# Gating a result one product later in the mix stage, and VectorE kept to the written order of these steps

## The chip, the core and the metric

The kernel runs on one core of a Trainium2 chip. The metric is the device time of one execution in microseconds (us), and the time of a kernel is the median of its runs. The engines that matter here are TensorE (PE in the profile; PEld is its loading of weights), VectorE (DVE), ScalarE (ACT), GpSimd (POOL), and SyncE (SP, whose queue issues nearly all of the transfers; SPq is that queue). PSUM is the memory that TensorE adds its products into, in eight banks of 128 x 512 fp32.

## What is computed

One layer of a decoder, 2048 rows of 1024 fp32 values. Two mixers read the same modulated input, their gated results are merged, projected and normalized:

```
a = sliding_window_sink_attention(q, k, v, ...) * silu(a_gate);  a = a @ w_attn_proj
p = pooled(p_in) * pool_scale * silu(p_gate);                    p = p @ w_pool_proj
y = sigmoid(m_a) * a + sigmoid(m_p) * p
y = (y @ w_out) * (1 + gate)
x = layer_norm(alpha * x + y, gain, bias)
```

The change lies in the third of these lines: in the products with `w_attn_proj` and `w_pool_proj`, and in the multiplications with sigmoid(m_a) and sigmoid(m_p) that use up their results.

## The kernel before

**Products.** Every fp32 matrix is held as a high part and a low part in TensorE's fp32r type, and a product is three passes: high by high, high by low, low by high. A *quad* is two blocks of 128 output columns by two halves of 512 rows, computed by a scheme of seven block products instead of eight. They are called B11, T1, T2, B21, T3, B22 and T4 after the set of input sums that each reads (`sets[name]`). Each is twelve matmuls of 128x128 by 128x512. A quad accumulates in three PSUM banks: a and b (tag `mm`, four banks) and c (tag `lg`, two banks).

**Groups.** Quads go through TensorE in pairs, called a group: x0 and x1. `front` writes B11 and T1 of both quads. `back` then writes T2 and B21 of x0, T2 and B21 of x1, T3 and B22 of x0, T3 and B22 of x1, T4 of x0 and T4 of x1; then the next group's `front` follows. So a group is fourteen products. A step called `tick` stands behind each product; it counts them, and starts what was put off with `defer(n, ...)`.

**Additions and results.** Between the products VectorE does two additions for each quad: b = c + p5 behind T2 (line 368), and p5 = c + p5 behind T3 (line 390). The latter reads the bank c that T4 goes on writing, so T4 of that quad can't start before it. A quad gives four results, at different times: *a* after B21, *p* (the sum p5) after T3, *b* after B22, *c* after T4. Where a result is complete, `q.consume` is called. In the text below x1's results carry a prime: a', p', b', c'.

**The mix stage.** It begins at about 1180 us and has these parts: attention projection for the first 1024 rows (s=0), pool projection for s=0, attention for s=1, pool for s=1, each of two groups of two quads, and then the output projection with the normalization. In the attention parts `consume` (line 618) is one VectorE multiplication of the result by its gate tile, into a tile `wide` in SBUF. In the pool parts it is a multiplication (line 627, into the gate's own tile g) and an addition to `wide` (line 629), and the sum is stored to `y_d` in DRAM, on SP's queue, three ticks later.

**Weights.** Each quad's raw weights are loaded on SP's queue. GpSimd forms three sums of blocks (`sum1`, line 269; `mid`, lines 273 and 274; `late`, line 278), ScalarE casts the high part (line 306, tile `w_set`), and VectorE subtracts it from the raw weights to give the low part (line 132, `w_set<-W`, 128x1024 for two products; `w_set<-A`, 128x512, for T4 alone). `mid` of a quad overwrites weights that the low part of its first pair reads, so it follows that subtraction. The low part that the next group's first product B11 of x0 needs, in its last four matmuls, is called **first low part** below.

**Sets.** In each part the next part's input sums are loaded and split too: ScalarE casts, VectorE subtracts (`set_B<-set_B`, `set_T<-set_T`, 128x1024), fourteen such steps for each part, mostly in its second group.

**What sets the order.** Each engine runs one fixed list of instructions. Those lists are made before the run, by a scheduler that starts from the written order and may move an instruction that has no data dependence. An instruction that is issued through `dve`, `act`, `pool`, `pe` or `sp` (objects of the class `Ordered`) is kept behind the instruction that was written just before it on its engine; one that is issued through `nc.vector` and so on is free.

Of the kernel before, what the change touches and what calls it, by code (L numbers as in the profile page):

```python
# [15 lines left out]
ALU = mybir.AluOpType  # L16
# [7 lines left out]
CH = 512  # L24
# [36 lines left out]
def kernel(  # L61
# [22 lines left out]
    nc = tc.nc  # L84
    pe, act, dve, pool, sp = (Ordered(tc, e) for e in (nc.tensor, nc.scalar, nc.vector, nc.gpsimd, nc.sync))
# [37 lines left out]
    y_d = dp.tile([2, KT, 2, P, CH], F32, name="y_d")  # L123
# [18 lines left out]
    def bank(tag="mm"):  # L142
        return ps.tile([P, CH], F32, tag=tag, bufs={"mm": 4, "lg": 2, "pt": 1, "pv": 1}[tag], name=tag)
# [160 lines left out]
    def pair_split(ph, raw, a=nc.scalar, d=nc.vector):  # L304
        hi, lo = ph.split(), ph.split()
        a.copy(by_two(hi), raw)  # L306
        low(d, by_two(lo), raw, by_two(hi))
        return halves(hi, lo)

    def half_split(ph, raw):  # L310
        s = ph.split()
        hi, lo = s[:, 0:CH], s[:, CH:]
        nc.scalar.copy(hi, raw)
        low(nc.vector, lo, raw, hi)
        return hi, lo

    def product(acc, w, name, first=False, i0=0, i1=4):
        t = sets[name]
        hi, lo = w
        for n, (part, u) in enumerate(((hi, 0), (hi, 1), (lo, 0))):  # L320
            for i in range(i0, i1):
                mm(
                    acc,
                    part[:, i * P : (i + 1) * P],
                    t[:, i, u, :],
                    start=first and i == 0 and n == 0,
                    stop=i == 3 and n == 2,
                    skip_group_check=True,
                )
# [11 lines left out]
    def back(ph, grp, opened, nxt, own, tick):  # L341
        st = []
        for q in grp:
            if q.ahead:
                q.ahead(ph, 0)
                defer(2, lambda q=q: q.ahead(ph, 1))
        for q, (a, b, c, w, *copy) in zip(grp, opened):
            p5 = None if copy else ph.p("p5")
            if w is None:
                c = bank("lg")  # L350
                nc.scalar.copy(c, a)
                nc.scalar.copy(p5, b)
                w = pair_split(ph, q.second())[::-1]
                q.late()
                product(c, w[1], "T2")
            elif copy:
                p5 = copy[0]
            else:
                u2 = ph.p("u2")
                nc.scalar.copy(u2, a)  # L360
                if c is None:
                    c = bank("lg")
                    product(c, w[1], "T2", True)
                nc.vector.tensor_tensor(c, c, u2, ALU.add)
                nc.scalar.copy(p5, b)
            tick()
            if len(copy) < 2:
                nc.vector.tensor_tensor(b, c, p5, ALU.add)
            if not copy:
                product(a, w[0], "B21")  # L370
            tick()
            q.consume(ph, 0, 0, a)
            st.append((q, b, c, p5))
        w = {}

        def ask(q):

            defer(1, lambda: q.load(ph, own, nc.sync, None))
            defer(3, lambda: q.sum1(nc.gpsimd))

        def third(x):
            w[x] = opened[x][5] if len(opened[x]) > 5 else pair_split(ph, st[x][0].third())[::-1]
            if x < len(nxt):
                ask(nxt[x])

        def with_t3(x):
            q, b, c, p5 = st[x]
            product(c, w[x][1], "T3")
            tick()
            nc.vector.tensor_tensor(p5, c, p5, ALU.add)  # L390
            q.consume(ph, 1, 1, p5)

        def with_b22(x):
            q, b, c, p5 = st[x]
            product(b, w[x][0], "B22")
            tick()
            q.consume(ph, 0, 1, b)

        for x in range(len(st)):
            third(x)  # L400
            with_t3(x)
            with_b22(x)
        for q in nxt[len(st) :]:
            ask(q)
        for q, b, c, p5 in st:
            w = half_split(ph, q.a22)
            product(c, w, "T4")
            tick()
            q.consume(ph, 1, 0, c)

    def finish_pairs(ph, grp, opened, tick):

# [41 lines left out]
    def defer(ticks, f):  # L454
        due.append((now[0] + ticks, len(due), f))
# [140 lines left out]
    def wide(ph, i):  # L596
        return ph.t.tile([P, D], F32, tag=f"wide{i}", bufs=1, name=f"wide{i}")

    def gates_ahead(name, s, m, raw):
        g = {}  # L600

        def ahead(ph, turn):
            for mi, t in (((0, 0), (1, 1)), ((0, 1), (1, 0)))[turn]:
                x = g[mi, t] = ph.c("g")
                sp.dma_start(x, gates_d[name][s, m + mi, t])
                if raw:
                    nc.scalar.activation(x, x, AF.Sigmoid)

        return g, ahead

    def attn_quad(s, m):
        g, ahead = gates_ahead("ma", s, m, True)

        def consume(ph, mi, t, src):
            k = m + mi
            if k not in ta:
                ta[k] = wide(ph, k)
            nc.vector.tensor_tensor(ta[k][:, t * CH : (t + 1) * CH], src, g.pop((mi, t)), ALU.mult)

        return Quad((wap[m], wap[m + 1]), consume, ahead)  # L620

    def pool_quad(s, m):
        gates, ahead = gates_ahead("mp", s, m, True)

        def consume(ph, mi, t, src):
            g = gates.pop((mi, t))
            nc.vector.tensor_tensor(g, src, g, ALU.mult)
            dst = ta[m + mi][:, t * CH : (t + 1) * CH]
            nc.vector.tensor_tensor(dst, g, dst, ALU.add)
            defer(3, lambda: sp.dma_start(y_d[s, m + mi, t], dst))  # L630

        return Quad((wpp[m], wpp[m + 1]), consume, ahead)

    zs = {}

# [878 lines left out]
    def rooms_of(name, dt=F32):  # L1514

        q = [kvp.tile([P, D], dt, tag=f"qs{i // 2}{i % 2}", name=f"{name}_qs{i}") for i in range(4)]
        k = kvp.tile([P, 2 * (P + 2 * CH)], F32, tag="kk", name=f"{name}_kk")
        v = kvp.tile([P, (2 * NB + 1) * P], F32, tag="vv", name=f"{name}_vv")
        return q, k, v
# [22 lines left out]
    with Pools("g0", spare=2, p=2, c=5) as ph:  # L1542
        started = head(ph, plans[0])
        kq, k, v = rooms_of("first", F32R)
# [7 lines left out]
    with Pools("g1", spare=4, p=2, c=5) as ph:  # L1552
        kq, k, v = rooms_of("second")
# [6 lines left out]
    ta, vec = {}, {}  # L1560
    with Pools("mix", spare=4, p=2, c=8) as ph:
# [3 lines left out]
        for s in range(2):  # L1565
            phases.append((pairs(lambda m, s=s: attn_quad(s, m)), ain_d[s]))
            phases.append((pairs(lambda m, s=s: pool_quad(s, m)), pin_d[s]))
# [86 lines left out]
```

## Time and profile before

| | us |
|---|---|
| median of 3 runs | 1693.23 |
| lowest and highest run | 1687.39, 1694.29 |
| the profiled execution | 1693.3 |
| its span, first to last instruction | 1691.5 |
| TensorE busy | 1648.7 (97% of the span) |
| VectorE busy | 1193.7 (71%) |
| ScalarE busy | 1030.0 (61%) |
| GpSimd busy | 988.5 (58%) |

How such rows are read. A row of the timeline is: start in us from the span's start, duration in us, engine, line, operation, output <- inputs, shapes, and the count of merged instructions. What stands in brackets is the engine's idle time ahead of the row, and what ended it. Rows of one engine may overlap by some hundredths. A table by stretches gives for each engine the busy time and, in brackets, the number of instructions; behind them stand the granted TensorE clock (1.00 is full), the share of the transfer engines and GB/s. Many steps are recorded by helper functions and then have the helper's line, 57; there the tile's name tells them apart.

### The profile page before, as it was taken

The page shows a single profiled execution, that of the slowest core. Times are in us where ns is not written, and L with a number is a line of the kernel's source. Part 1 is how long each engine was busy: PE and PEld are TensorE (multiplying, and loading weights), DVE is VectorE, ACT ScalarE, POOL GpSimd, SP SyncE. Part 2 cuts the span into 40 slices and gives each one's busy share as a digit, 9 for nine tenths or more (in the row PEclk, how much of TensorE's full clock was granted, in tenths as well). Part 3 has the DMA queues.
Part 4 walks back from the last instruction along what each step waited for, and adds up shares of the span by engine and source line. Part 5 has one row for each costly group of instructions (what it writes and reads, how often), then busy time and mean ns, then how long its engine had stood idle before and what let it go on. Part 6 is the DMA issues. An engine that isn't in the chain of part 4 may idle for free.

```text
span 1691.5 us, 24675 instructions
## 1 busy us (share of the span) xinstructions
PE 1648.7 (97%) x8058; PEld 1384.4 (82%) x8058; DVE 1193.7 (71%) x2132; ACT 1030.0 (61%) x2150; POOL 988.5 (58%) x734
## 2 busy tenths in 40 slices
PE   7999999999999999999999999999999999999997
PEld 6788888888888888888788888888878777887886
DVE  6856545676857657357567677676669897989877
ACT  4755457878778755335578777876646445644452
POOL 3343437586857828762476867496567576533442
PEclk9999999999999999999999999999999999999999
DMA  9688843343432478766533344234979797888443
GB/s 359 219 279 307 197 161 102 101 132 108 149 107 99 135 248 308 267 231 211 190 114 99 114 130 156 81 114 135 336 247 363 262 360 259 318 283 271 150 150 112
DMA packets 188849, 336.79 MB, mean 199 GB/s; under 512 B 18336, under 2 KB 44080, under 8 KB 188720
## 3 DMA queue, kind: packets, MB, share of 16 engines
q1 hardware_dynamic: 185600, 330.96, 57.3%
q10 hardware_dynamic: 3088, 4.23, 1.0%
q8 instruction: 64, 1.05, 0.2%
q14 instruction: 65, 0.53, 0.1%
q0 software_dynamic: 32, 0.02, 0.0%
HBM read 227.96 MB, written 110.33 MB: 200 GB/s over the span
## 4 chain that ended last, share of the span: by engine, by line
PE 74%; DVE 8%; DMA 7%; ACT 4%; issue 3%; POOL 3%; SPq 1%; POOLq 0%; DVEq 0%; ACTq 0%
PE mm L57 48%; PE lg L57 19%; PE pv L57 4%; PE pt L57 4%; DVE w_set L132 1%; DMA ain_T<-spare 1%; ACT L L57 1%; DMA g<-ma_d 1%; DMA g<-mp_d 1%; DVE w_set L57 1%; DVE set_T L57 1%; POOL W L269 1%; DMA spare<-pin_B 1%; DVE L L57 1%; ACT w_set L57 1%
## 5 line engine op out<-in xcount | busy, mean ns | idle before, releaser
L57 PE MATMUL mm<-set_B,w_set 128*128 128x512 f32 x2664 | 655.8, 393 | 2.2 <-DVE w_set L132 1.2
L57 PEld LDWEIGHTS mm<-set_B,w_set 128*128 128x128 f32 x2664 | 497.1, 189 | 107.0 <-DVE w_set L132 2.4
L57 PE MATMUL mm<-set_T,w_set 128*128 128x512 f32 x1824 | 455.5, 396 | 5.9 <-DVE mm L57 3.9
L57 PE MATMUL lg<-set_T,w_set 128*128 128x512 f32 x1704 | 412.6, 392 | 10.5 <-DVE p L390 4.4
L57 PEld LDWEIGHTS mm<-set_T,w_set 128*128 128x128 f32 x1824 | 336.7, 189 | 76.2 <-DVE mm L57 6.5
L57 PEld LDWEIGHTS lg<-set_T,w_set 128*128 128x128 f32 x1704 | 319.9, 189 | 81.8 <-ACT w_set L306 5.2
L132 DVE TENSOR_TENSOR w_set<-W,w_set 128x1024 fp32r<-128x1024 f32 x137 | 197.8, 1445 | 142.3 <-ACT w_set L306 129.3
L306 ACT CAST w_set<-W 128x1024 fp32r<-128x1024 f32 x137 | 143.8, 1050 | 212.7 <-PE mm L57 124.3
L57 POOL TENSOR_TENSOR w_set<-W,w_set 128x512 fp32r<-128x512 f32 x120 | 157.3, 1318 | 116.9 <-ACT w_set L57 112.0
L269 POOL TENSOR_TENSOR W<-W,A 128x512 f32<-128x512 f32 x46 | 74.1, 1610 | 232.5 <-DMA A<-in_win_dram 63.5
L57 DVE TENSOR_TENSOR o<-pv,o 64x128 f32<-64x128 f32 x256 | 72.1, 282 | 133.7 <-ACT o L57 127.3
L57 POOL TENSOR_TENSOR spare<-spare 128x512 f32<-128x512 f32 x68 | 124.0, 1826 | 31.5 <-DMA spare<-pin_B 12.2
L57 POOL TENSOR_TENSOR W<-W 128x512 f32<-128x512 f32 x82 | 108.3, 1336 | 53.2 <-DVE sm L57 31.0
L57 ACT ACTIVATE L<-L,nm 128x257 f32<-128x257 f32 (+1 forms) x256 | 127.2, 499 | 9.3 <-DVE nm L57 3.7
L278 POOL TENSOR_TENSOR W<-W 128x512 f32<-128x512 f32 x46 | 72.8, 1583 | 95.9 <-DVE w_set L132 83.5
L57 DVE CUSTOM_DVE_ANT_0 L<-lg,bt,nsink 128x256 f32<-128x256 f32 (+1 forms) x256 | 111.7, 473 | 21.3 <-PE lg L57 11.9
L57 ACT CAST w_set<-W 128x512 fp32r<-128x512 f32 (+1 forms) x165 | 101.4, 628 | 20.9 <-POOL W L57 14.9
L273 POOL TENSOR_TENSOR W<-W 128x512 f32<-128x512 f32 x44 | 72.7, 1656 | 66.3 <-DVE w_set L132 57.2
L57 ACT COPY o<-pv 64x256 f32<-64x256 f32 x128 | 47.4, 370 | 75.9 <-PE pv L57 74.7
L57 DVE TENSOR_TENSOR ptl<-pt,pth 128x512 fp32r<-128x512 f32 (+1 forms) x128 | 85.7, 669 | 1.3 <-ACT pth L57 1.0
L274 POOL TENSOR_TENSOR W<-W 128x512 f32<-128x512 f32 x44 | 71.6, 1628 | 21.9 <-DMA W<-in_win_dram 18.9
L57 ACT ACTIVATE L<-L,sm 128x256 f32<-128x256 f32 (+1 forms) x128 | 64.3, 502 | 31.7 <-DVE sm L57 31.4
(230 smaller groups left out, 2398.2 us busy)
## 6 DMA issues: line engine op xcount, KB each, us to landing
W<-in_win_dram SPq DMA_DIRECT2D x42, 512.0 KB, 5.4
W<-in_win_dram SPq DMA_DIRECT2D x42, 256.0 KB, 3.7
A<-in_win_dram SPq DMA_DIRECT2D x42, 256.0 KB, 4.9
ag_d<-sig SPq DMA_DIRECT2D x32, 256.0 KB, 5.7
pg_d<-sig SPq DMA_DIRECT2D x32, 256.0 KB, 4.4
pg<-pg_d SPq DMA_DIRECT2D x32, 256.0 KB, 3.2
pin_B<-fin SPq DMA_DIRECT2D x32, 256.0 KB, 2.0
ag<-ag_d SPq DMA_DIRECT2D x32, 256.0 KB, 2.9
```

The costliest lines, as they stand in the source:

```text
L57: return lambda *args, **kw: self.tc.keep_in_program_order(op(*args, **kw))
L132: engine.tensor_tensor(dst, src, as32(hi), ALU.subtract)
L269: e.tensor_tensor(self.w[:, 1, :], self.w[:, 2, :], self.a22, ALU.add)
L273: e.tensor_tensor(x[:, 1, :], x[:, 1, :], x[:, 0, :], ALU.subtract)
L274: e.tensor_tensor(x[:, 2, :], x[:, 0, :], x[:, 2, :], ALU.subtract)
L278: e.tensor_tensor(x[:, 3, :], x[:, 3, :], x[:, 1, :], ALU.subtract)
L306: a.copy(by_two(hi), raw)
```

## The change

The results of the attention and pool quads go through `one_behind`: `consume` now first does the gating of the result that came before, and keeps its own for the next call. The last result of a group is done one tick after its T4 is written (`defer(1, use_up)`). The store of a pool result to `y_d` is deferred by two ticks instead of three. The gatings, and in these quads the two additions of `back`, are issued through `dve` instead of `nc.vector`. No instruction is added and none is taken away.

```diff
@@ back
-                nc.vector.tensor_tensor(b, c, p5, ALU.add)
+                (dve if q.ahead else nc.vector).tensor_tensor(b, c, p5, ALU.add)
...
-            nc.vector.tensor_tensor(p5, c, p5, ALU.add)
+            (dve if q.ahead else nc.vector).tensor_tensor(p5, c, p5, ALU.add)
             q.consume(ph, 1, 1, p5)
...
             product(c, w, "T4")
             tick()
             q.consume(ph, 1, 0, c)
+        defer(1, use_up)
...
+    unused = []
+
+    def use_up():
+        while unused:
+            unused.pop()()
+
+    def one_behind(use):
+
+        def consume(ph, mi, t, src):
+            use_up()
+            unused.append(lambda: use(ph, mi, t, src))
+
+        return consume
...
-            nc.vector.tensor_tensor(ta[k][:, t * CH : (t + 1) * CH], src, g.pop((mi, t)), ALU.mult)
+            dve.tensor_tensor(ta[k][:, t * CH : (t + 1) * CH], src, g.pop((mi, t)), ALU.mult)
-        return Quad((wap[m], wap[m + 1]), consume, ahead)
+        return Quad((wap[m], wap[m + 1]), one_behind(consume), ahead)
...
-            nc.vector.tensor_tensor(g, src, g, ALU.mult)
+            dve.tensor_tensor(g, src, g, ALU.mult)
             dst = ta[m + mi][:, t * CH : (t + 1) * CH]
-            nc.vector.tensor_tensor(dst, g, dst, ALU.add)
-            defer(3, lambda: sp.dma_start(y_d[s, m + mi, t], dst))
-        return Quad((wpp[m], wpp[m + 1]), consume, ahead)
+            dve.tensor_tensor(dst, g, dst, ALU.add)
+            defer(2, lambda: sp.dma_start(y_d[s, m + mi, t], dst))
+        return Quad((wpp[m], wpp[m + 1]), one_behind(consume), ahead)
```

What it does to the engines' lists: those of TensorE and ScalarE stay as they are. VectorE's changes within the four attention and pool parts, GpSimd's at one place, SP's by some rows of `y_d` stores.

**VectorE, first group of the pool part for s=0, from the low part of T4's weights to the first low part of the next group.** Before (g_13484 and wide0 gate and add the result b; p5_13498 is x1's sum; g_13434 and wide3 are for p', g_13490 and wide2 for b'; w_set_13672 is the first low part):

```order
L132 TENSOR_TENSOR w_set_13625<-A22_13237,w_set_13625 128x512
L627 TENSOR_TENSOR g_13484<-mm_13352,g_13484 128x512
L132 TENSOR_TENSOR w_set_13652<-A22_13287,w_set_13652 128x512
L629 TENSOR_TENSOR wide0_12869<-g_13484,wide0_12869 128x512
L390 TENSOR_TENSOR p5_13498<-lg_13499,p5_13498 128x512
L627 TENSOR_TENSOR g_13434<-p5_13498,g_13434 128x512
L629 TENSOR_TENSOR wide3_12984<-g_13434,wide3_12984 128x512
L627 TENSOR_TENSOR g_13490<-mm_13390,g_13490 128x512
L132 TENSOR_TENSOR w_set_13672<-W_13559,w_set_13671 128x1024
L629 TENSOR_TENSOR wide2_12911<-g_13490,wide2_12911 128x512
```

Now (what is issued through `dve` has line 57; wide1 adds the result p, w_set_13670 is the first low part):

```order
L132 TENSOR_TENSOR w_set_13623<-A22_13236,w_set_13623 128x512
L57 TENSOR_TENSOR wide1_12958<-g_13428,wide1_12958 128x512
L132 TENSOR_TENSOR w_set_13650<-A22_13286,w_set_13650 128x512
L57 TENSOR_TENSOR p5_13496<-lg_13497,p5_13496 128x512
L57 TENSOR_TENSOR g_13484<-mm_13351,g_13484 128x512
L57 TENSOR_TENSOR wide0_12909<-g_13484,wide0_12909 128x512
L57 TENSOR_TENSOR g_13434<-p5_13496,g_13434 128x512
L57 TENSOR_TENSOR g_13490<-mm_13390,g_13490 128x512
L57 TENSOR_TENSOR wide3_12997<-g_13434,wide3_12997 128x512
L57 TENSOR_TENSOR wide2_12943<-g_13490,wide2_12943 128x512
L132 TENSOR_TENSOR w_set_13670<-W_13556,w_set_13669 128x1024
```

x1's sum p5 now stands ahead of the gating of b, and the first low part stands behind one instruction more, the addition of b'.

**VectorE, second group of the pool part for s=1, from the middle of the group.** Before (w_set_15152 is the low part of x1's third pair, which T3 and B22 of x1 read; g_15001 and wide4 are for a, g_15007 and wide6 for a', p5_15013 is x0's sum):

```order
L627 TENSOR_TENSOR g_15001<-mm_14936,g_15001 128x512
L368 TENSOR_TENSOR mm_14971<-lg_15062,p5_15061 128x512
L629 TENSOR_TENSOR wide4_14447<-g_15001,wide4_14447 128x512
L57 TENSOR_TENSOR set_B11_66<-set_B11_66 128x2x512
L627 TENSOR_TENSOR g_15007<-mm_14970,g_15007 128x512
L629 TENSOR_TENSOR wide6_14491<-g_15007,wide6_14491 128x512
L132 TENSOR_TENSOR w_set_15152<-W_14870,w_set_15151 128x1024
L390 TENSOR_TENSOR p5_15013<-lg_15014,p5_15013 128x512
```

Now (g_15001 and wide4 are for a again; w_set_15150 is the low part, p5_15013 x0's sum):

```order
L57 TENSOR_TENSOR g_15001<-mm_14934,g_15001 128x512
L57 TENSOR_TENSOR wide4_14489<-g_15001,wide4_14489 128x512
L132 TENSOR_TENSOR w_set_15150<-W_14868,w_set_15149 128x1024
L57 TENSOR_TENSOR p5_15013<-lg_15014,p5_15013 128x512
L57 TENSOR_TENSOR g_15007<-mm_14970,g_15007 128x512
L57 TENSOR_TENSOR set_T2_234<-set_T2_234 128x2x512
L57 TENSOR_TENSOR wide6_14516<-g_15007,wide6_14516 128x512
```

The gating and the addition of a' stood ahead of this low part and of x0's sum, and now stand behind both. In the second group of the pool part for s=0 they stood ahead of x0's sum, and now stand behind it; and in both second groups the first low part now stands behind two instructions more, the addition of b' and the gating of c.

**GpSimd, second group of the pool part for s=0, with the weights of the next attention group (W_13877 and W_13923 before are x0's and x1's).** Before:

```order
L274 TENSOR_TENSOR W_13877<-W_13877 128x512
L57 TENSOR_TENSOR spare_13831<-spare_13830,spare_13831 128x512
L273 TENSOR_TENSOR W_13877<-W_13877 128x512
L269 TENSOR_TENSOR W_13923<-W_13923,A22_13924 128x512
```

Now (W_13874 and W_13921):

```order
L274 TENSOR_TENSOR W_13874<-W_13874 128x512
L57 TENSOR_TENSOR spare_13829<-spare_13828,spare_13829 128x512
L269 TENSOR_TENSOR W_13921<-W_13921,A22_13922 128x512
L57 TENSOR_TENSOR spare_13828<-spare_13828 128x512
L274 TENSOR_TENSOR W_13921<-W_13921 128x512
L273 TENSOR_TENSOR W_13874<-W_13874 128x512
```

`sum1` of x1 no longer stands behind the half of x0's `mid` (line 273) that follows the first low part.

## The prediction

> **What bounds the kernel now.** I read the page's first part, the table of stretches, the waits of TensorE in the stage that changes, and then TensorE's timeline there, product by product.
>
> ```profile
> span 1691.5 us, 24675 instructions
> PE 1648.7 (97%) x8058; PEld 1384.4 (82%) x8058; DVE 1193.7 (71%) x2132; ACT 1030.0 (61%) x2150; POOL 988.5 (58%) x734
> ...
> 1300.00:1400.00 100.00, 96.08 (x413) 78.15 (x413) 93.13 (x81) 49.39 (x66) 66.07 (x35) 0.98 0.88 314
> ...
> PE lg L57 <- DVE p L390: 4.4, 3, 2.2
> ```
>
> TensorE is the bound, with 97% of the span. VectorE comes near it only in the mix stage: 93% from 1300 to 1400 us. There it holds TensorE up, as in the last row: three waits for the sum p5, 4.4 us together. The next rows are TensorE's, at the six places of the four parts where it loses more than a tenth of a microsecond or two.
>
> ```profile
> 1234.77 1.99 PE L57 MATMUL lg<-set_T,w_set 128*128 128x512 f32 x8
> 1240.75 2.07 PE L57 MATMUL lg<-set_T,w_set 128*128 128x512 f32 x4 [4.00 <-DVE w_set L132]
> ...
> 1247.02 5.60 PE L57 MATMUL lg<-set_T,w_set 128*128 128x512 f32 x24
> ...
> 1320.46 2.88 PE L57 MATMUL mm<-set_B,w_set 128*128 128x512 f32 x12
> 1323.18 2.88 PE L57 MATMUL lg<-set_T,w_set 128*128 128x512 f32 x12
> 1328.30 4.48 PE L57 MATMUL lg<-set_T,w_set 128*128 128x512 f32 x12 [2.24 <-DVE p L390]
> ...
> 1335.36 2.88 PE L57 MATMUL mm<-set_T,w_set 128*128 128x512 f32 x12
> ...
> 1370.72 1.97 PE L57 MATMUL mm<-set_B,w_set 128*128 128x512 f32 x8
> 1373.74 1.20 PE L57 MATMUL mm<-set_B,w_set 128*128 128x512 f32 x4 [1.04 <-DVE w_set L132]
> ...
> 1378.27 3.02 PE L57 MATMUL mm<-set_B,w_set 128*128 128x512 f32 x12 [0.62 <-ACT w_set L306]
> ...
> 1405.93 2.88 PE L57 MATMUL lg<-set_T,w_set 128*128 128x512 f32 x12
> 1409.48 3.00 PE L57 MATMUL lg<-set_T,w_set 128*128 128x512 f32 x12 [0.67 <-DVE p L390]
> ...
> 1415.50 2.90 PE L57 MATMUL mm<-set_T,w_set 128*128 128x512 f32 x12
> ...
> 1489.33 3.12 PE L57 MATMUL mm<-set_B,w_set 128*128 128x512 f32 x12
> 1492.28 2.89 PE L57 MATMUL mm<-set_T,w_set 128*128 128x512 f32 x12
> ...
> 1522.21 2.88 PE L57 MATMUL lg<-set_T,w_set 128*128 128x512 f32 x12
> 1526.57 2.98 PE L57 MATMUL lg<-set_T,w_set 128*128 128x512 f32 x12 [1.48 <-DVE p L390]
> ...
> 1532.12 2.88 PE L57 MATMUL mm<-set_T,w_set 128*128 128x512 f32 x12
> ```
>
> Undisturbed, a product takes 2.72 us (1320.46 to 1323.18), so 0.227 a matmul, 1.81 for its first eight, 0.91 for its last four. Start to start, less 2.72 for each product between, the places lose:
> - place 1 (attention, s=0, first group): 12.25 - 5.44 = 6.8
> - place 2 (pool, s=0, first group): from T4 of x0 to T1, 12.18 - 8.16 = 4.0
> - place 3 (pool, s=0, second group, and the fronts behind it): 7.55 - 5.44 = 2.1
> - place 4 (attention, s=1, first group): 9.57 - 8.16 = 1.4
> - place 5 (pool, s=1, first group): 2.95 - 2.72 = 0.2
> - place 6 (pool, s=1, second group): 9.91 - 8.16 = 1.75
>
> Together 16.3 us, 1% of the time. No gain of the change can be more. Part of it is clock, not waiting: behind the 2.24 us wait at place 2 twelve matmuls took 4.48 instead of 2.88, 1.6 more, with the granted clock at 0.72 of full speed:
>
> ```profile
> 1326.00:1332.00 6.00, 3.76 (x11) 2.96 (x11) 5.93 (x7) 1.04 (x1) 2.80 (x3) 0.72 0.97 334
> ```
>
> At place 1 a wait of 4.00 lost 6.8, so 2.8 more; at place 6 a wait of 1.48 cost nothing more (2.98 for twelve). I price a new wait so: under 2 us as it is, about 2.2 with 1.6 on top, about 4 with 2.8 on top.
>
> The sum goes against the profiled execution, 1693.3 us (1691.5 of span and 1.8 around it); the median of the three runs, 1693.23, is the same.
>
> **The change, part by part.** No instruction comes or goes, and the lists of TensorE and ScalarE stand still. So all that counts is when VectorE gives out two things: x1's sum p5, for which T4 waits, and the first low part, for which the next group's first product waits after eight matmuls. Outside the four parts nothing moves. The waits from 1150 us to the end name only one of TensorE's behind place 6, so what is won or lost by then stays:
>
> ```profile
> PE lg L57 <- DVE mm L435: 0.2, 1, 0.2
> ```
>
> *Place 1: 0.* Ahead of the low part that TensorE waits for (at 1240.75) the list has the same instructions, in another order.
>
> *Place 2: -2.25.*
>
> ```profile
> 1324.10 0.68 DVE L627 TENSOR_TENSOR g<-mm,g 128x512 f32<-128x512 f32 x1
> ...
> 1325.81 1.75 DVE L629 TENSOR_TENSOR wide<-g,wide 128x512 f32<-128x512 f32 x1
> 1327.48 0.68 DVE L390 TENSOR_TENSOR p<-lg,p 128x512 f32<-128x512 f32 x1
> ...
> 1330.48 1.21 DVE L132 TENSOR_TENSOR w_set<-W,w_set 128x1024 fp32r<-128x1024 f32 x1
> 1331.61 0.68 DVE L629 TENSOR_TENSOR wide<-g,wide 128x512 f32<-128x512 f32 x1
> ```
>
> The gating and the addition of b, 0.60 and 1.67 start to start, now stand behind x1's sum. It ends 2.27 earlier, at 1325.9, just when T4 of x0 ends (1323.18 + 2.72). So the wait and its clock go, 4.0 us. But VectorE is busy without a gap here, and the first low part, which ended at 1331.6, gets b''s addition ahead of it (0.60): 1332.2. The first product now starts at 1328.6, has done eight matmuls at 1330.4, waits 1.8, and ends at 1332.2 + 0.91 = 1333.1 instead of 1335.36. Bounds: -4.0, if the new wait doesn't arise; -0.65, if its 1.8 us lower the clock (1.6).
>
> *Place 3: +4.5.*
>
> ```profile
> 1357.32 0.69 DVE L390 TENSOR_TENSOR p<-lg,p 128x512 f32<-128x512 f32 x1 [0.23 <-PE lg L57]
> ...
> 1372.47 1.21 DVE L132 TENSOR_TENSOR w_set<-W,w_set 128x1024 fp32r<-128x1024 f32 x1
> ...
> 1375.41 1.73 POOL L269 TENSOR_TENSOR W<-W,A 128x512 f32<-128x512 f32 x1
> ...
> 1377.17 1.05 ACT L306 CAST w_set<-W 128x1024 fp32r<-128x1024 f32 x1 [10.84 <-POOL W L269]
> ```
>
> VectorE came to x0's sum with 0.23 us to spare, waiting for T3. The gating and the addition of a' (0.6 each) now stand behind that sum, so it waits 1.2 longer and has them still to do. b''s addition and c's gating (0.6 each) come ahead of the first low part too. It ended at 1373.6; now 1376.0 or so. TensorE takes its last four matmuls up 2.4 later (1373.74 before), and after a wait of 3.5, since its first eight are done at 1372.5; by the nearest row, 4.00, the clock adds 2.8. Against that, GpSimd's `sum1` of x1, which ended at 1377.1 and let ScalarE start at 1377.17, no longer stands behind x0's `mid`: TensorE's 0.62 us wait goes. 2.4 + 2.8 - 0.7 = 4.5. Bounds: -2.1, if the low part comes in time; +7.7, if three additions that move into GpSimd's work take 1.75 instead of 0.68, as the two `wide` rows at place 2 show (+3.2).
>
> *Place 4: -1.4.*
>
> ```profile
> 1412.59 0.69 DVE L618 TENSOR_TENSOR wide<-lg,g 128x512 f32<-128x512 f32 x1 [1.33 <-PE lg L57]
> 1413.20 1.22 DVE L132 TENSOR_TENSOR w_set<-W,w_set 128x1024 fp32r<-128x1024 f32 x1
> ```
>
> x1's sum has one multiplication fewer ahead of it (0.6, the wait was 0.67), and the first low part no longer stands behind the gating of c', which had to wait 1.33 for T4. Both waits go. Bounds: -1.4 to 0, if VectorE comes late out of place 3.
>
> *Place 5: +0.4.*
>
> ```profile
> 1489.99 1.21 DVE L132 TENSOR_TENSOR w_set<-W,w_set 128x1024 fp32r<-128x1024 f32 x1
> ```
>
> The first low part ended at 1491.1; with b''s addition ahead of it at 1491.7, and the product 0.91 later at 1492.6, against 1492.28. Bounds: -0.2 to +0.8.
>
> *Place 6: +2.3.*
>
> ```profile
> 1514.01 1.23 DVE L132 TENSOR_TENSOR w_set<-W,w_set 128x1024 fp32r<-128x1024 f32 x1 [0.99 <-ACT w_set L306]
> ...
> 1529.53 1.21 DVE L132 TENSOR_TENSOR w_set<-W,w_set 128x1024 fp32r<-128x1024 f32 x1
> ```
>
> x1's sum has the gating and the addition of b and one low part fewer ahead of it, so T4 starts in time and the next product at 1522.21 + 5.44 = 1527.65; it wants the first low part at 1529.5. That ended at 1530.7. VectorE idled 0.99 for ScalarE ahead of x1's third pair; a''s two steps (1.2) now stand behind that, so the idle time grows by them; b''s addition and c's gating (1.2) come ahead. 1533.1, if all additions keep their lengths; the long ones here had met GpSimd at work, and if one or two fall elsewhere, 1.1 each, 1531.0 to 1532.0. I take 1531.9: a wait of 2.4, priced like the 2.24, and T1 starts at 1531.9 + 0.9 + 1.6 = 1534.4 instead of 1532.12. Bounds: -1.75 to +4.7 (1533.1, 2.8 of clock).
>
> The stores to `y_d` are written at the same tick as before, and SP has them behind a weight load or two where they stood ahead. In this part one load of `y_d` rows, weights for x1 of the first output group, waits behind the store of a''s sum, which comes up to 4 us later:
>
> ```profile
> 1525.17 1.04 ACT L306 CAST w_set<-W 128x1024 fp32r<-128x1024 f32 x1 [2.57 <-PE lg L57]
> ...
> 1534.84 2.88 PE L57 MATMUL mm<-set_B,w_set 128*128 128x512 f32 x12
> ```
>
> The high part of these weights was ready at 1526.2, 8.6 us ahead of the product that reads it, so 0.
>
> Sum: 0 - 2.25 + 4.5 - 1.4 + 0.4 + 2.3 = +3.55; 1693.3 + 3.55 = 1696.9 us.
>
> One rule speaks against the clock's part of it. The Trainium skill, on the page "TensorE: Matmul & The Clock Gate", in the section "Why this matters for your kernels", has throughput drop only after TensorE gaps of more than about 3 us. By it the wait at place 6 would add no clock (the one at place 3 would), and the sum would be 1695.3. The trace differs: 2.24 us were enough.
>
> **The rivals.**
> - *Slower: VectorE's late low parts grow.* At places 3 and 6 the first low part comes 4 us or more after it is wanted, because the moved additions meet GpSimd. For it: VectorE is 93% busy there, and `wide` additions took 1.75 as well as 0.68. Against it: when TensorE is late, VectorE catches up. All upper bounds: -0.65 + 7.7 + 0 + 0.8 + 4.7 = +12.6, 1705.9 us. It is slower by 0.5% from +8.5 on, so when places 3 and 6 together cost some 10.
> - *Faster: the sums come early and nothing takes their place.* All lower bounds: -4.0 - 2.1 - 1.4 - 0.2 - 1.75 = -9.5, 1683.8 us. For it: the waits on p5 are the most frequent here. Against it: the first low part has more ahead of it at places 2, 3, 5 and 6, never less but at place 4.
> - *The clock stays at full speed.* Then the new waits cost only themselves: 3.55 - 2.8 - 1.6 = -0.85, 1692.5 us. For it: 1.48 us left no mark; against it: 2.24 did.
> - *The change doesn't order anything that matters,* as an instruction is held only behind the one written before it: 1693.3 us. Against it: VectorE's list differs in all four parts.
>
> **How the numbers follow.** 0.5%, or 8.5 us, is about what a measurement of this kernel can tell from no change; its runs spread by 6.9. Chances: the forecast 0.40, the slower rival 0.28, the faster one 0.10, the clock at full speed 0.14, nothing ordered 0.08. Only the first two rivals pass 8.5 us, so faster 0.10, within 0.5% 0.62, slower 0.28. The time is the forecast's, 1696.9. The range goes from 1686, which leaves out most of the faster case, to 1706, all upper bounds: about 0.8.
>
> **What would show it.** Right: place 2's wait for p5 gone and one of 1 to 2 us for `w_set` in the fronts; at places 3 and 6 waits of `mm` for `w_set` line 132 of 2 to 4 us with a lowered clock behind them; place 1 as before; `sum1` ahead of line 273 at place 3. Wrong: no wait of TensorE's fronts over 1 us (then the faster rival), or waits over 4 us there (then the slower one). What I can't see is how GpSimd's work falls against VectorE's new order; that would make the sizes wrong first.

## The result, and the profile after

The changed kernel took 1698.1 us in the median of 16 runs (1691.5 to 1703.3), the kernel before 1689.3 in 16 runs beside them (1685.7 to 1694.3). The ratio is 1.0045, with a 95% interval of 1.0033 to 1.0058. On another occasion the same two kernels gave 1695.2 (12 runs) and 1691.0 (29 runs), ratio 1.0026 (1.0012 to 1.0039). So the change makes the kernel slower by a quarter to a half per cent: 4 and 8 us by the two ratios, 4.3 and 8.8 us between the medians.

The profiled execution took 1693.87 us, 4 us less than its median; that of the kernel before, 1693.3, lies as much above its own. The two profiles therefore differ by less than the kernels do, and this needs an explanation of its own (the experiment that runs the changed kernel again). First the page of the changed kernel, and the waits of TensorE from 1150 us to the end, longest in the last column:

```profile
span 1692.1 us, 24681 instructions
PE 1646.7 (97%) x8058; PEld 1384.8 (82%) x8058; DVE 1190.9 (70%) x2132; ACT 1031.2 (61%) x2150; POOL 987.6 (58%) x734
```

```profile
PE mm L57 <- DVE w_set L132: 7.8, 2, 5.5
PE lg L57 <- DVE w_set L132: 4.7, 2, 3.9
PE lg L57 <- ACT w_set L306: 0.3, 1, 0.3
PE lg L57 <- DVE mm L436: 0.2, 1, 0.2
```

The three waits for p5 are gone. In their place stand waits of `mm` for line 132, 7.8 us in two: the first low part, at places 3 and 6. TensorE's timeline in the changed kernel at places 1, 2, 3 and 6:

```profile
1239.08 1.19 PE L57 MATMUL lg<-set_T,w_set 128*128 128x512 f32 x4 [3.90 <-DVE w_set L132]
...
1315.21 1.98 PE L57 MATMUL lg<-set_T,w_set 128*128 128x512 f32 x8
1317.94 1.21 PE L57 MATMUL lg<-set_T,w_set 128*128 128x512 f32 x4 [0.76 <-DVE w_set L132]
...
1327.19 3.29 PE L57 MATMUL mm<-set_B,w_set 128*128 128x512 f32 x12
...
1365.69 1.97 PE L57 MATMUL mm<-set_B,w_set 128*128 128x512 f32 x8
1373.19 2.07 PE L57 MATMUL mm<-set_B,w_set 128*128 128x512 f32 x4 [5.52 <-DVE w_set L132]
...
1520.12 5.60 PE L57 MATMUL lg<-set_T,w_set 128*128 128x512 f32 x24
1525.56 1.98 PE L57 MATMUL mm<-set_B,w_set 128*128 128x512 f32 x8
1529.82 1.55 PE L57 MATMUL mm<-set_B,w_set 128*128 128x512 f32 x4 [2.28 <-DVE w_set L132]
```

At place 6 the two T4s now follow each other without a gap (24 matmuls in 5.60 us) and the next product stops behind its eighth matmul, as forecast. At place 3 the wait is 5.52 us.

For all kernels below, this is what each place loses in its profiled execution. It is worked out from the starts of TensorE's matmuls in the trace: a stretch of 84 matmuls (seven products) takes 19.04 us undisturbed; what it took beyond that is the loss. "4" holds the group behind place 3 too. "Sum" is over the 17 such stretches that hold the four parts. It has losses elsewhere in them too: 0.4 to 1.1 us in most rows, but 6.9 in `both` and 3.0 in `both2`, mostly around the end of the second attention group of s=0.

```
                 1      2      3      4      5      6    sum
before         6.9    4.0    2.3    1.8    0.5    1.8   17.8
after          5.9    1.5    7.6    0.0    0.0    4.2   19.8
after_again    3.2    2.0    6.8    0.0    0.0    5.1   17.6
attn_only      5.9    2.8    2.3    0.7    0.0    3.9   16.0
pool_s0        6.3    1.4    9.3    0.6    0.5    1.9   20.4
pool_s1        7.2    6.0    1.7    1.8    0.0    3.9   21.3
order_only     5.7    2.2    2.1    1.5    0.0    2.1   14.0
delay_only     6.1    4.3    1.8    1.8    0.0    1.5   16.6
low_first      7.0    1.4    2.1    2.6    0.0    1.2   14.8
filled         6.8    1.1    5.3    0.0    0.0    3.0   16.7
both           0.2    0.0    2.0    1.5    0.0    0.3   10.9
attn1          0.3    3.5    2.3    1.2    0.1    1.1    9.2
both2          0.2    1.9    2.3    1.4    0.0    2.9   11.7
```

A row is one execution. A kernel's executions differ by 4 to 13 us, so the rows say where time goes, and the intervals below say how much. The changed kernel's two rows, 19.8 and 17.6, lie 2.0 above and 0.2 under that of the kernel before; neither shows the 4 to 8 us.

### The profile page after: what moved, and what is told of

It reads as the page before. It is cut to its first block, busy times and chain, and to the rows that moved or that the text cites. A ratio compares the mean times of both kernels' runs of the same rounds, so it can differ in the third digit from the quotient of the medians.

```text
span 1692.1 us, 24681 instructions
## 1 busy us (share of the span) xinstructions
PE 1646.7 (97%) x8058; PEld 1384.8 (82%) x8058; DVE 1190.9 (70%) x2132; ACT 1031.2 (61%) x2150; POOL 987.6 (58%) x734
## 4 chain that ended last, share of the span: by engine, by line
PE 73%; DVE 9%; DMA 9%; issue 3%; ACT 3%; POOL 2%; SPq 1%; POOLq 0%; DVEq 0%; ACTq 0%
PE mm L57 48%; PE lg L57 18%; PE pv L57 4%; PE pt L57 4%; DVE w_set L132 2%; DMA set_T<-ain_T 2%; DVE set_T L57 1%; DVE wide L57 1%; DMA head_T<-in_wada_dram 1%; ACT L L57 1%; DMA g<-mp_d 1%; DVE w_set L57 1%; DVE L L57 1%; DMA A<-wmix_d 1%; DMA set_B<-pin_B 1%
```

## The experiments

My theory: the change wins the waits for p5 and pays with the first low part, which comes late at places 3 and 6, and with the clock that falls behind these waits. All times are medians; the ratio is to the kernel before, run beside.

**One part of the change alone.** `attn_only` has it in the attention parts, `pool_s0` and `pool_s1` in the pool part of one half. The edit, for the pool quads of one s (the additions of `back` go through `dve` where `q.kept`):

```diff
-            dve.tensor_tensor(g, src, g, ALU.mult)
+            v = dve if s == 0 else nc.vector
+            v.tensor_tensor(g, src, g, ALU.mult)
...
-            defer(2, lambda: sp.dma_start(y_d[s, m + mi, t], dst))
+            defer(2 if s == 0 else 3, lambda: sp.dma_start(y_d[s, m + mi, t], dst))
-        return Quad((wpp[m], wpp[m + 1]), one_behind(consume), ahead)
+        return Quad((wpp[m], wpp[m + 1]), one_behind(consume) if s == 0 else consume, ahead, s == 0)
```

> The change is kept in the attention parts alone; the pool parts are as before. Late-low-part theory (the cost sits at places 3 and 6, where the first low part of the next group has more ahead of it): nothing of the cost is here; place 1 keeps its loss of about 6 to 7 us, place 4's 1.4 us go, so -1.4 us against the kernel before. Rival (holding VectorE to the written order costs by itself, wherever it is done): half of the measured 8.8 us would show here, some +4 us.

> The change is kept in the two groups of the pool part for s=0 alone. Late-low-part theory: place 2 loses 1.3 instead of 4.0 us (-2.7) and place 3 loses 7.5 instead of 2.1 (+5.4), so +2.7 us against the kernel before; TensorE's wait for line 132 behind the first eight matmuls at place 3 is 5 to 6 us. If the 8.8 us between the medians all arise here, +7 or more. Rival (place 3's wait comes from the stores to y_d or from the late start after place 2, not from VectorE's list): the wait stays near 1 us and the time is 2 to 3 us under the kernel before.

> The change is kept in the two groups of the pool part for s=1 alone. Late-low-part theory: the wait of 1.48 us for the sum at place 6 goes, a wait of about 2.3 us for line 132 takes its place with a lowered clock behind it, place 6 loses 4.2 instead of 1.75 us: +2.4 us. Rival (place 6 is only late because places 2 and 3 disturbed what comes before it): place 6 loses under 1 us, and the time is 1 to 2 us under the kernel before.

Measured: `attn_only` 1689.7, ratio 0.9987 (0.9975 to 0.9999); `pool_s0` 1694.2, 1.0011 (0.9996 to 1.0026); `pool_s1` 1695.0, 1.0023 (1.0012 to 1.0034). In us of 1691 that is -2.2, +1.9 and +3.9; the interval of `pool_s0` holds 1. The attention parts cost nothing, so holding VectorE to the written order is not a price wherever it is done. `pool_s0` wins at place 2 and loses at place 3, `pool_s1` trades its wait at place 6 for another:

```profile
1367.67 1.98 PE L57 MATMUL mm<-set_B,w_set 128*128 128x512 f32 x8
1375.71 2.08 PE L57 MATMUL mm<-set_B,w_set 128*128 128x512 f32 x4 [6.06 <-DVE w_set L132]
```

(place 3 of `pool_s0`), and at place 6 of `pool_s1`:

```profile
1527.31 1.98 PE L57 MATMUL mm<-set_B,w_set 128*128 128x512 f32 x8
1531.33 1.95 PE L57 MATMUL mm<-set_B,w_set 128*128 128x512 f32 x4 [2.04 <-DVE w_set L132]
```

Both rivals about the pool parts fall: the wait at place 3 did not stay near 1 us, and place 6 loses 3.9 although VectorE's list at places 2 and 3 is that of the kernel before. In `pool_s1` the lists of TensorE, ScalarE and GpSimd are those of the kernel before throughout, so only VectorE's order and the stores can be what costs there, and the stores are tried by the next experiment. The three ratios add up to +0.21%, 3.6 us, near the lower of the two measurements of the whole.

**One half of the change alone.** `order_only` issues through `dve` and delays nothing, the stores keep their three ticks; `delay_only` delays, has the stores at two ticks, and issues through `nc.vector`. Each edit is against the changed kernel.

```diff
@@ order_only
-            defer(2, lambda: sp.dma_start(y_d[s, m + mi, t], dst))
+            defer(3, lambda: sp.dma_start(y_d[s, m + mi, t], dst))
-        return Quad((wpp[m], wpp[m + 1]), one_behind(consume), ahead)
+        return Quad((wpp[m], wpp[m + 1]), consume, ahead)
...
@@ delay_only
-            dve.tensor_tensor(g, src, g, ALU.mult)
+            nc.vector.tensor_tensor(g, src, g, ALU.mult)
...
```

> Half of the change: the gatings and the two additions are issued through dve, but each result is gated at once and the stores keep their three ticks. VectorE's list at places 2, 3 and 6 is then that of the kernel before but for a swap or two. Theory that the cost comes from what the two halves do together to the list: within 2 us of the kernel before, with the waits for p5 of L390 back (about 2.2 and 1.5 us at places 2 and 6) and waits for line 132 at places 3 and 6 under 1.5 us. Rival (to hold VectorE to the written order costs by itself): +4 us or more.

> The other half: the gating of a result is written one product later and the stores after two ticks, but all is issued through nc.vector, so the scheduler may move it. It does: at places 1 and 2 the list is that of the kernel before. Theory that both halves are needed: within 2 us of the kernel before, waits for p5 back. Rival (the later writing costs, by stores that come later or by gates that are held longer): +4 to +9 us as in the changed kernel.

Measured: `order_only` 1691.9, 0.9996 (0.9985 to 1.0007); `delay_only` 1690.1, 0.9994 (0.9983 to 1.0004). Neither half costs anything that can be told from zero; the cost needs both. Alone, the written order is nearly the order that the scheduler had chosen anyway: by the names in the traces six of VectorE's instructions stand elsewhere. A delay alone is largely undone by the scheduler, which moves the gatings forward again; around place 2 the list is that of the kernel before. The waits for the sums are back in `order_only`:

```profile
PE lg L57 <- DVE p L57: 4.3, 3, 1.9
```

In `delay_only` the wait at place 2 (2.35 us) is put down to ScalarE's cast of weights, which ended 0.1 us behind the sum; T4 can't start before the sum, as before.

**The first low part ahead of what is left over.** `low_first` is the whole change, but b', c and c' are gated behind the next group's first low part.

```diff
         while unused:
-            unused.pop()()
+            unused.pop(0)()
...
         def consume(ph, mi, t, src):
-            use_up()
+            if (mi, t) != (1, 0):
+                use_up()
```

> The whole change, but the results that are left when a group ends (b', c and c') are gated behind the next group's first low part instead of ahead of it. Late-low-part theory: the waits for the sums p5 are gone as in the changed kernel and the waits for line 132 at places 2, 3 and 6 shrink to under 1.5 us each; places 2, 3, 4 and 6 together lose 2 to 5 us instead of 13 in the changed kernel (9.3 before): 8 to 11 us under the changed kernel, 4 to 7 us under the kernel before. Rival (the low part is late because VectorE as a whole has too much work there, whatever the order): the waits stay, or come back as waits for the result banks that the late gating frees, and the time stays within 2 us of the changed kernel.

Measured: 1690.3, ratio to the kernel before 0.9998 (0.9989 to 1.0007). Against the changed kernel's two ratios it is 5 to 8 us faster, so the order around the first low part is what costs. (ScalarE's and GpSimd's lists change at some places too; but in `pool_s1` the cost came with both as they were.) Place 3, VectorE in the changed kernel: x0's sum and the set split behind it, then all from x1's sum to the first low part:

```profile
1352.29 0.69 DVE L57 TENSOR_TENSOR p<-lg,p 128x512 f32<-128x512 f32 x1 [0.56 <-PE lg L57]
...
1354.22 2.32 DVE L57 TENSOR_TENSOR set_T<-set_T 128x1024 fp32r<-128x1024 f32 x1
...
1361.10 0.68 DVE L57 TENSOR_TENSOR p<-lg,p 128x512 f32<-128x512 f32 x1
1361.70 1.27 DVE L57 TENSOR_TENSOR g<-mm,g 128x512 f32<-128x512 f32 x2
1362.90 1.24 DVE L57 TENSOR_TENSOR wide<-g,wide 128x512 f32<-128x512 f32 x1
1364.06 2.30 DVE L57 TENSOR_TENSOR set_T<-set_T 128x1024 fp32r<-128x1024 f32 x1
1366.29 1.77 DVE L57 TENSOR_TENSOR g<-p,g 128x512 f32<-128x512 f32 x1
1367.98 3.42 DVE L57 TENSOR_TENSOR wide<-g,wide 128x512 f32<-128x512 f32 x2
1371.32 0.68 DVE L57 TENSOR_TENSOR g<-lg,g 128x512 f32<-128x512 f32 x1
1371.92 1.21 DVE L132 TENSOR_TENSOR w_set<-W,w_set 128x1024 fp32r<-128x1024 f32 x1
```

and in `low_first`, from x1's sum on:

```profile
1363.10 0.68 DVE L57 TENSOR_TENSOR p<-lg,p 128x512 f32<-128x512 f32 x1
1363.70 0.68 DVE L57 TENSOR_TENSOR g<-mm,g 128x512 f32<-128x512 f32 x1
1364.41 1.73 DVE L57 TENSOR_TENSOR wide<-g,wide 128x512 f32<-128x512 f32 x1
1366.07 2.31 DVE L57 TENSOR_TENSOR set_T<-set_T 128x1024 fp32r<-128x1024 f32 x1
1368.30 1.77 DVE L57 TENSOR_TENSOR g<-p,g 128x512 f32<-128x512 f32 x1
1369.99 2.30 DVE L132 TENSOR_TENSOR w_set<-W,w_set 128x1024 fp32r<-128x1024 f32 x1
```

10.8 us from the sum to the low part became 6.9, since the additions of p' and b' (3.4 us) and the gatings of b' and c now stand behind it. Places 3 and 6 lose 2.1 and 1.2 instead of 7.6 and 4.2. But 8 to 11 us under the changed kernel and 4 to 7 us under the kernel before, which I expected, did not come: place 1 keeps its 7 us, and at place 4 x1's sum and the gatings of b and p' now stand ahead of T4's low parts, for which a new wait of 1.68 us arises.

**The clock.** `filled` is the whole change with 16 matmuls more inside the wait at place 3 and 8 more at place 6. They go to a bank that nothing reads; all of the computation is there. Up to place 3 all lists are the changed kernel's; behind it ScalarE's, VectorE's and GpSimd's differ by some swaps, from which no new wait arises.

```diff
-        product(a, w[0], "B11", True)
+        if fill:
+            product(a, w[0], "B11", True, parts=(0, 1))
+            spare = bank("pt")
+            for i in range(fill):
+                mm(spare, w[0][0][:, 0:P], sets["B11"][:, i % 4, 0, :], start=True, stop=True, skip_group_check=True)
+            product(a, w[0], "B11", False, parts=(2,))
+        else:
+            product(a, w[0], "B11", True)
...
```

> The whole change, and 16 matmuls more at place 3 and 8 more at place 6, between the eighth and the ninth matmul of the first product of x0, into a bank that nothing reads: 3.6 and 1.8 us of TensorE work inside the waits for the first low part (5.5 and 2.3 us). Nothing of the computation is left out. Theory that a lowered clock is a good part of the cost: no time at the lowered clock at these two places (10.2 us of it at half speed in the changed kernel's profile, 5.1 us lost), the first low part as late as before, so 3.5 to 5 us under the changed kernel. Rival (the wait alone is the price): within 1.5 us of the changed kernel.

Measured: 1694.0, ratio 1.0015 (1.0002 to 1.0028), 2 to 5 us under the changed kernel's two ratios. Place 3 in it, and the stretches at places 3 and 6 with the granted clock (third number from the end):

```profile
1367.57 1.98 PE L57 MATMUL mm<-set_B,w_set 128*128 128x512 f32 x8
1369.38 3.79 PE L57 MATMUL pt<-set_B,w_set 128*128 128x512 f32 x16
1374.53 1.21 PE L57 MATMUL mm<-set_B,w_set 128*128 128x512 f32 x4 [1.36 <-DVE w_set L132]
```

```profile
1366.00:1380.00 14.00, 12.64 (x56) 10.12 (x55) 14.00 (x11) 5.05 (x6) 10.75 (x7) 1.00 0.66 224
1525.00:1535.00 10.00, 9.16 (x41) 7.27 (x40) 10.00 (x12) 4.63 (x6) 3.37 (x2) 1.00 1.00 355
```

The low part is still 5 us late, but no time passes at a lowered clock, and places 3 and 6 lose 8.3 instead of 11.8 and 11.9. So in these profiles about a third of the price of these waits is clock. By the runs the filling won back 2 to 5 of the 4 to 8 us, and the mean granted clock went back with it: 0.9965 for the kernel before (35 runs), 0.9937 and 0.9945 for the changed one (16 and 12), 0.9966 for `filled` (12). An estimate from these means: of the 8.8 and 4.3 us between the medians at most 4.7 and 3.4 are clock (0.0028 and 0.0020 of 1692 us).

**The changed kernel again.** No edit.

> The changed kernel once more, for a second profile: the first one's execution (1693.87 us) lies 4 us under the median of its runs, the kernel before's 4 us above its own. Theory that the rest of the 8.8 us between the medians is the clock, which is lowered for a different time from run to run: 6 to 9 us over the kernel before, and in a profile near the median the same waits (5 to 6 us at place 3, about 2 at place 6) with more than the 13.6 us at the lowered clock that the first profile has between 1200 and 1560 us, or longer waits at places 1 to 6. Rival (the difference lies outside the four parts): the four parts take the 343.4 us that they took in the first profile, and the rest is longer.

Measured: +4.3 us instead of the 6 to 9 expected. The rival falls: behind the four parts the second profile has 146.7 us to the end, as the first had, and the four parts begin at 1202.7 us here and 1202.0 there. The four parts took 341.3 us here and 343.4 there, with much the same wait at place 3 (4.9 us here) and a longer one at place 6 (3.3 instead of 2.3). What differs most is place 1, 3.2 against 5.9: the wait is 2.30 us here instead of 3.90, and the twelve matmuls behind it run at full clock, in 2.89 us:

```profile
1238.65 1.19 PE L57 MATMUL lg<-set_T,w_set 128*128 128x512 f32 x4 [2.30 <-DVE w_set L132]
1239.68 2.89 PE L57 MATMUL mm<-set_B,w_set 128*128 128x512 f32 x12
```

In its 16 runs the changed kernel's time rises by 2.1 us for each 0.001 of mean clock that is missing, and a straight line through them takes up 60% of the scatter. So a lower clock goes with much of the scatter, and with the distance between profile and median: the first profile has 0.995 against a mean of 0.9937, that of the kernel before 0.994 against 0.9965. Waits and lowered clock come together in these runs, so the line doesn't tell them apart. The theory stays untried: the second profile lies under its median again, and has 6.8 us at half clock in the four parts where the first has 13.6. What a median execution of the changed kernel looks like stays open, and so does where all of its 4 to 8 us lie.

**A version that is faster than both.** `both` puts `low_first`'s order into the pool parts, and in the attention parts writes the low part of x1's third pair ahead of T3 of x0, and those for the T4s ahead of T3 and B22 of x1. `attn1` is `attn_only` with these earlier low parts at place 1 alone, `both2` is `both` with them at place 1, and at place 4 those for the T4s only.

```diff
...
             third(x)
+            if x == 0 and len(st) > 1 and st[0][0].kept:
+                w[1] = pair_split(ph, st[1][0].third())[::-1]
+            if x == 1 and st[0][0].kept:
+                h.append(half_split(ph, st[0][0].a22))
             with_t3(x)
+            if x == 1 and st[0][0].kept:
+                h.append(half_split(ph, st[1][0].a22))
             with_b22(x)
...
```

> The pool parts as in low_first (results left at a group's end gated behind the next first low part), and in the attention parts the low part of x1's third pair is written ahead of T3 of x0, and the low parts for the T4s ahead of T3 and B22 of x1, so that they stand earlier in VectorE's list. Theory that where a low part stands in VectorE's list is what decides at every place: place 1's wait of 4 us falls to under 2 us and its loss from 6.8 us to 3 or less, places 2, 3, 4 and 6 lose under 6 together; 6 to 9 us under the kernel before. Rival (VectorE has too much work at place 1, so another low part or sum is late in its place): place 1 still loses 5 us or more, and the time is within 3 us of the kernel before.

> As attn_only, and at place 1 alone (the first attention group of s=0) the low part of x1's third pair is written ahead of T3 of x0, and the low parts for the T4s ahead of T3 and B22 of x1. The second groups keep their order, in which the kernel named both gained a new loss of 5.3 us. Theory that where the low part stands decides: places 1 and 4 lose under 1 us together instead of 8.2, so 7 to 8 us under the kernel before. Rival (what TensorE wins it gives back later, as the 2.7 us won at place 2 were given back at place 3): place 2 or the groups between lose what was won, and the time is within 3 us of the kernel before.

> The pool parts as in low_first; in the attention parts the earlier low parts only where they help: at place 1 all of them, at place 4 those for the T4s. Places 1, 2 and 4 lose under 1.5 us together, place 3 with the group behind it 3 to 4, place 6 about 1, so some 10 to 12 us are won of the 16.3 that the kernel before loses: 7 to 12 us under it by the runs. Rival (VectorE's amount of work, not its order, is the bound from 1300 us on): the waits move to the groups behind, and the time is that of both, 2 us under the kernel before.

Measured: `both` 1689.3, 0.9988 (0.9978 to 0.9998); `attn1` 1686.4, 0.9973 (0.9963 to 0.9984); `both2` 1685.5, 0.9965 (0.9951 to 0.9979). The last two are faster than either kernel, 4.5 and 5.4 us under the kernel before. Place 1, the largest loss of the kernel before, is gone in all three; in `attn1`:

```profile
1235.11 3.08 PE L57 MATMUL lg<-set_T,w_set 128*128 128x512 f32 x12
```

`both` was 2 us under the kernel before where I expected 6 to 9. It gave most of its gain back, 5.3 us, at the end of the second attention group: TensorE came to the next group's first product 4.4 us earlier than in the kernel before, but the first low part started no earlier (at 1288.89, before at 1289.01). In `attn1`, where the second group keeps its order, 0.2 us are lost there. In `both`:

```profile
1290.63 1.31 PE L57 MATMUL mm<-set_B,w_set 128*128 128x512 f32 x4 [2.47 <-DVE w_set L132]
1291.74 4.43 PE L57 MATMUL mm<-set_T,w_set 128*128 128x512 f32 x12
```

`attn1` fell short of what I expected (7 to 8) by 2.5 to 3.5 us, `both2` (7 to 12) by 1.6 at least; its places 1, 2, 4 and 6 lost 6.4 where I expected some 2.5. I had taken the gains from one profile of the kernel before, an execution above its median, whose 6.9 us at place 1 hold 2.8 us of lowered clock. That this is what the rest went to was not tried by itself.

## Why the prediction was right, and where its steps were not

I forecast 1696.9 us; the two measurements, 1698.1 and 1695.2, lie on both sides of it. The mechanism was right: the waits for p5 go, the first low part takes their place at places 3 and 6, with a lowered clock behind it, and `low_first` and `pool_s1` show that this is what costs. The difference that I gave, +3.55, is near the second measurement (+4.3) and under the first (+8.8). That the time came out so near is partly luck: my sum stood on an execution of 1693.3, 2 to 4 us over the medians that the kernel before then had. Nor do the terms add up to it: as measured below they give +1.9 us in the first profile and -0.1 in the second, not +3.55. So the places and the kind of wait are borne out, the size of the whole only by the medians. By the terms:

- *Place 1, 0:* -1.0 and -3.7 in the two profiles. The wait was 3.90 and 2.30; the list was reordered without cost, as said, and the rest is mostly clock.
- *Place 2, -2.25:* -2.5 and -2.0. The total was right and its parts were not. The wait for the first low part was not 1.8 us: the product lost 0.4. Another low part was late, that of x1's third pair (0.76 at 1317.94), since the gating and addition of a now stand right ahead of it. I had followed the list only from T4's low parts on.
- *Place 3, +4.5:* +5.3 and +4.5 in the two profiles. The wait was 5.5, not 3.5, and the clock added 1.8 (2.07 and 3.77 us for matmuls that take 1.20 and 2.88 at full clock), not 2.8. GpSimd's `sum1` came earlier and the wait of 0.62 went, as said. x0's sum starts 13.4 us ahead of TensorE's first product in both kernels (at 1357.32 before, at 1352.29 now). From it to the first low part VectorE needed 15.2 us before and needs 19.6 now, so the low part fell back by 4.5 instead of 2.4. The steps that I had moved, the gating and the addition of a', the addition of b' and the gating of c, take 3.6 of it: the addition of b' takes 1.7, which I had kept for the upper bound, and not 0.6. Another 1.1 is a set split, the one at 1354.22, which took 2.3 us in the changed kernel's first profile and 1.2 in that of the kernel before; I had kept the splits at one length.
- *Place 4, -1.4:* the waits went, -1.8 with the group ahead of it. `attn_only` won 2.2 us.
- *Place 5, +0.4:* -0.5. The low part came in time, so the sign was wrong.
- *Place 6, +2.3:* +2.4 and +3.4; in the first profile the wait of 2.28 and its clock, 1.6, are what I had written (2.4 and 1.6), in the second the wait was 3.3.
- *The price of the clock by the length of a wait* is the step that failed in kind. It is told below.

The stores to `y_d` were costed at nothing, and nothing speaks against it: `delay_only` has them at two ticks and costs nothing. The rival in which the low parts grow was nearer than its 0.28 let one think. A wait over 4 us was my sign for it, and at place 3 it was 5.5 and 4.9 us; at place 6, with 2.3 and 3.3, it was the forecast's; and the first measurement, +8.8 between the medians and 0.45% by its ratio, lies at the 8.5 us or 0.5% from which I counted the rival. For those 8.5 places 3 and 6 would have had to cost some 12 with the other terms as forecast, not the 10 that I wrote; they cost 7.7 and 7.9.

## What to carry to other kernels

Where an engine is nearly always busy, to bring one of its results forward is to put another back, so follow every result that somebody waits for through the whole group, with the long and the short form of each step, and not only the one whose wait is to go. A delay and a fixed order may each be harmless where a scheduler can repair the other, and cost when both are set. Where the waits are of the order of 2 us, sum up against several executions, since a wait of one length may or may not be followed by a lowered clock, which costs up to 1.7 us for each stretch of 3.41.

## What was not expected of the hardware

The granted clock does not go by the length of a wait. In each profile it changes only at multiples of 3.41 us from the clock's first record: in the kernel before it stood at full for 238.93 us, at half for 3.41, at full for 976.21, at half for 6.83, at full for 81.92, at half for 3.41, which are 70, 1, 286, 2, 24 and 1 times 3.413. In the 13 profiles each stretch of that grid in the four parts that ran at full clock and in which TensorE was busy for 1.51 us or less is followed by one at half clock (20 stretches), and none with 1.56 or more. So the time at which a wait falls decides. In these rows PE's busy time is the first number behind the length, and the clock the third from the end. The kernel before, at place 2, behind a wait of 2.24 us:

```profile
1324.70:1328.10 3.40, 1.36 (x7) 0.78 (x5) 3.40 (x4) 1.04 (x1) 3.05 (x3) 1.00 0.99 324
1328.10:1331.50 3.40, 3.20 (x8) 2.55 (x9) 3.33 (x5) 0.00 (x0) 0.58 (x1) 0.50 1.01 366
```

`attn1` at the same place, with a longer wait that falls into two stretches:

```profile
1323.27 2.99 PE L57 MATMUL lg<-set_T,w_set 128*128 128x512 f32 x12 [2.84 <-DVE p L391]
```

```profile
1318.70:1322.10 3.40, 1.72 (x7) 0.81 (x5) 3.40 (x4) 0.10 (x1) 3.32 (x3) 1.00 0.96 340
1322.10:1325.50 3.40, 2.23 (x10) 1.88 (x11) 3.33 (x6) 0.95 (x1) 1.55 (x1) 1.00 1.01 375
```

And the border, in `after_again` at place 3 (1.56 busy, the clock stays; 0.31, it falls) and in `attn_only` at place 6 (1.46, it falls):

```profile
1364.50:1367.90 3.40, 1.56 (x7) 0.94 (x6) 3.40 (x3) 1.04 (x1) 3.40 (x3) 1.00 0.14 52
1367.90:1371.30 3.40, 0.31 (x1) 0.30 (x2) 3.40 (x4) 0.00 (x0) 2.23 (x3) 1.00 0.53 166
1371.30:1374.70 3.40, 3.40 (x9) 2.64 (x8) 3.33 (x5) 1.53 (x2) 2.24 (x2) 0.50 0.90 299
```

```profile
1522.30:1525.70 3.40, 1.46 (x6) 1.24 (x7) 3.33 (x5) 1.02 (x1) 0.64 (x1) 1.00 1.04 404
1525.70:1529.10 3.40, 3.40 (x9) 2.64 (x8) 3.40 (x5) 1.04 (x1) 0.61 (x1) 0.50 0.91 272
```

The border does not hold everywhere. Ahead of the four parts, in the kernel before and in `both`, a stretch with 2.0 us of work was followed by one at half clock:

```profile
256.30:259.70 3.40, 1.98 (x11) 1.25 (x10) 0.63 (x4) 3.33 (x6) 2.16 (x2) 1.00 0.30 111
259.70:263.10 3.40, 3.40 (x10) 2.63 (x9) 0.15 (x1) 1.92 (x7) 3.32 (x4) 0.50 0.00 0
```

The change has no part in that stretch of the kernel before, and it made the four parts begin some 1.6 us later there than in the first profile of the changed kernel. So the two spans differ by 0.6 us only, although the four parts took 341.5 us before and 343.4 after. A stretch at half clock costs up to 1.7 us, half of 3.41, when TensorE has work throughout. This is why waits of 2.24 and 2.84 us have opposite prices; that it is also why one kernel's executions scatter is likely but not shown. The Trainium skill, on the page "TensorE: Matmul & The Clock Gate", in the section "Part 1: The HAM clock gate (the 'warmup' mystery)", says that the clock is set from a window of 3413 ns which runs freely and does not start with the kernel; the traces agree: the first record lies 20.4 to 23.8 us behind the span's start, from one profile to another. There I should have looked before pricing by length. The Trainium skill has, there too, the half clock follow an idle window; here a window that was idle for some 1.9 to 2.0 of its 3.4 us was enough.
